# Row sums and row arithmetic in the norms of a transformer kernel, with filler products behind them

## The chip, the cores and the metric

The kernel runs on one core of one Trainium2 chip. The metric is the time of one execution on the device in microseconds (us). It is compared with the time of the changed kernel on the same chip. The engines are named as the profile names them: PE is the matrix engine (PEld its weight loads), DVE the vector engine, ACT the scalar engine, POOL the general engine, and SP issues most DMAs. PSUM is the memory into which PE adds its products, SBUF the memory of everything else.

## The reference

Three transformer blocks in a row, for one sequence of 256 tokens with 1024 features:

```python
def layer_norm(x, g, b):
    mu = jnp.mean(xf, axis=-1, keepdims=True)
    var = jnp.mean(jnp.square(xf - mu), axis=-1, keepdims=True)
    y = (xf - mu) * lax.rsqrt(var + LN_EPS) * g.astype(jnp.float32) + b.astype(jnp.float32)
...
def rms_norm(x, g):
    y = xf * lax.rsqrt(jnp.mean(xf * xf, axis=-1, keepdims=True) + NORM_EPS)
...
# block 1
h = layer_norm(alpha * x + m @ w_out[i], ln1_g[i], ln1_b[i])
f = peer_ffn(h, peer_w_q[i], peer_sub_keys[i], peer_u[i], peer_v[i])
x = layer_norm(alpha * h + f + e, ln2_g[i], ln2_b[i])
# block 2, twice (NSA attention, then forgetting attention)
h = rms_norm(x, norm_g[i, 0])
x = x + rms_norm(m, norm_g[i, 1])
h = rms_norm(x, norm_g[i, 2])
x = x + rms_norm(squared_relu_mlp(h, mlp_w_up[i], mlp_w_down[i]), norm_g[i, 3])
# block 3, twice (mlstm with a gated MLP, then hgrn with a mixture of experts)
hn = rmsnorm(x, norm1_w[layer]) * (1 + scale1) + shift1
x = x + gate1 * y
hn = rmsnorm(x, norm2_w[layer]) * (1 + scale2) + shift2
x = x + gate2 * y
# end
return rmsnorm(x, final_norm_w)
```

Every norm needs, for each of the 256 tokens, the mean of 1024 squares and then one over its square root.

## The kernel before

Features lie on the partitions: an activation is eight tiles of 128 features x 256 tokens, so that a sum over features is a sum over partitions and tiles. A float32 weight is split into two parts (hi on ACT at L316, lo on DVE at L317, 128x1024 at a time), and a product with it is three products on PE (L327 to L329, in `mm3`): hi with hi, hi with the rest of the activation, and lo with hi. Weights come in through SP's queue. A scheduler places all instructions on their engines beforehand, and each engine then takes its own list in order. What follows a norm is therefore late when the norm is late.

A norm goes like this. `Squares.add` squares pairs of tiles on ACT and adds them up on DVE or POOL until two tiles of 128x512 are left. `fold` sums these over the partitions with eight products of one column each (L368): the squares of 128 tokens are the weights, and the result is one number for each token, 128 tokens down the partitions in two columns. `rstd` makes one over the root from these 128x2 numbers: ACT the square root (L376), DVE the variance times -0.5 (L377), the reciprocal (L378), and three more operations (L379 to L381), which are one step of Newton. `spread` (L391) turns the two columns into a row that stands in all partitions, 128x256 in PSUM, by two products. Then the eight tiles of the activation are multiplied with that row: at L453 in `layer_norm`, at L415 in `rms`, at L480 in `add_normed`, where ACT first copies the row to SBUF (L475).

Ten norms have this chain on the way to the next product: two of `layer_norm`, four of `add_normed`, three of `rms` (before mlstm, before its gated MLP, before hgrn), and the last of all. Four more norms are applied late (`inverse`): their products go on with the activation as it is, and the result is multiplied with the row behind. The router (`Router.finish`) uses the two columns as they are. The first layer norm stands at 270 us of the span, the second at 1200, the four of `add_normed` between 1389 and 1943 in attention and MLP in turn, mlstm's at 1942 and hgrn's at 2285, the router at 2473 and the last norm at 2907.

Of the kernel before, what the change touches and what calls it, by code (L numbers as in the profile page):

```python
# [22 lines left out]
T = 256  # L23
# [8 lines left out]
ADDS = 4  # L32
LNV = 8
EPS = (1e-6, 1e-5)
BASE = ("warm", "rs_v", "rs_r", "rs_t", "sqk", "yk", "sq2", "icol")

INV_FREQ = np.float32(10000.0) ** (-np.arange(0, 64, 2, dtype=np.float32) / np.float32(64))

# [178 lines left out]
class Core:  # L217
# [107 lines left out]
    def mm3(self, ps, w, x, start, stop, **k):  # L325
        mm = self.nc.tensor.matmul
        mm(ps, w[0], x[0], start=start, stop=False, **k)  # L327
        mm(ps, w[0], x[1], start=False, stop=False, **k)  # L328
        mm(ps, w[1], x[0], start=False, stop=stop, **k)  # L329

    def lin_chunk(self, src, x, kts=KT, apart=False):

# [61 lines left out]

    def rows_add(self, ps, x, first, last):

        self.nc.tensor.matmul(ps, self.C("onesD"), x, start=first, stop=last)

    def rstd_rows(self, sums, eps):
        return self.spread(self.ms_ps()[:, :T], self.rstd(sums[:, :2], eps))  # L400

    def squares(self, x):
        s = Squares(self)
# [1 line left out]
            s.add(x[:, 2 * j:2 * j + 2])  # L405
        return s

    def rms(self, x, sums, g, b=None, eps=1e-6):

        nc = self.nc  # L410
        r = self.rstd_rows(self.fold(sums), eps)
        hi, lo = self.big([KT, T], F32R, nm="nhi"), self.big([KT, T], F32R, nm="nlo")
        for k in range(KT):
            y = self.small([T], tag="yk", bufs=3)
            nc.vector.scalar_tensor_tensor(y, x[:, k], g[:, k:k + 1], r, op0=OP.mult, op1=OP.mult)  # L415
            if b is None:
                self.split(y, hi[:, k], lo[:, k])
            else:
                nc.scalar.activation(hi[:, k], y, AF.Identity, bias=b[:, k:k + 1])
                nc.vector.scalar_tensor_tensor(lo[:, k], y, b[:, k:k + 1], hi[:, k], op0=OP.add, op1=OP.subtract)  # L420
        return hi, lo
# [11 lines left out]
    def layer_norm(self, r, mean, g, b, g_next=None):  # L433


        nc = self.nc
        sq = Squares(self, nc.vector)
        for k in range(KT):
            nc.vector.tensor_tensor(r[:, k], r[:, k], mean, op=OP.subtract)
            if k % 2:  # L440
                sq.add(r[:, k - 1:k + 1])
        gh, bh = g, b
        if g_next is not None:
            gh, bh = (self.small([KT], tag=t, bufs=1) for t in ("gh", "bh"))
            nc.gpsimd.tensor_tensor(gh, g, g_next, op=OP.mult)
            nc.gpsimd.tensor_tensor(bh, b, g_next, op=OP.mult)
        rs = self.rstd_rows(self.fold(sq), 1e-5)
        hi, lo = (self.big([KT, T], F32R, nm="lhi"), self.big([KT, T], F32R, nm="llo"))
        sq = Squares(self)
        for k in range(KT):  # L450
            y = self.small([T], tag="yk", bufs=3)
            c = slice(k, k + 1)
            nc.vector.tensor_tensor(y, r[:, k], rs, op=OP.mult)  # L453
            nc.scalar.activation(hi[:, k], y, AF.Identity, scale=gh[:, c], bias=bh[:, c])
            eng = nc.vector if k < LNV else nc.gpsimd
            eng.tensor_scalar(r[:, k], y, g[:, c], b[:, c], op0=OP.mult, op1=OP.add)
# [11 lines left out]
    def add_normed(self, x, src, gm, sq, g=None):  # L468

        nc = self.nc
        r = self.rstd_rows(self.fold(sq), 1e-6)
        rs = self.small([T], tag="rsb", bufs=1)
        nc.scalar.activation(rs, r, AF.Copy)  # L475
        nxt = Squares(self, None if g is not None else nc.vector)
        parts = (self.big([KT, T], F32R, nm="nhi"), self.big([KT, T], F32R, nm="nlo")) if g is not None else None
        for k in range(KT):
            m = self.small([T], tag="yk", bufs=3)
            nc.vector.scalar_tensor_tensor(m, src(k), gm[:, k:k + 1], rs, op0=OP.mult, op1=OP.mult)  # L480
            eng = nc.vector if k < ADDS else nc.gpsimd
# [9 lines left out]
        self.nc.scalar.activation(hi, x[:, k], AF.Copy, scale=g[:, k:k + 1])  # L491
        self.nc.vector.scalar_tensor_tensor(lo, x[:, k], g[:, k:k + 1], hi, op0=OP.mult, op1=OP.subtract)  # L492

    def fold(self, sq):

        ps = self.sums()
        n = len(sq.tiles)
        for i, t in enumerate(sq.tiles):
            for f in range(2):
                self.add_sum(ps, 0, t[:, f], i + f == 0, i == n - 1 and f == 1, square=False)  # L500
        return ps

    def inverse(self, sums, eps=1e-6):

        r = self.rstd(sums[:, :2], eps)
        col, row = self.small([2], tag="icol", bufs=1), self.small([T], tag="irow", bufs=1)
        self.nc.vector.tensor_copy(col, r)
        self.nc.scalar.activation(row, self.spread(self.ms_ps()[:, :T], r), AF.Copy)
        return col, row

    def accumulate(self, w, hid, ys, first, last, dts=range(8)):

# [519 lines left out]
def squared_relu(c, x, sq, hs, l, g=None):  # L1032
# [2 lines left out]

    def evac(ps):
        r = c.small([2, T], tag="hr")
        row = inv[0][1][:, None, :].to_broadcast([128, 2, T])
# [53 lines left out]
def nsa(c, x, sq, hs):  # L1092
# [8 lines left out]
    kc, vc = kc[:, 0], kc[:, 1]  # L1101
    K2 = c.big([4, 2, T], nm="K2")
    ps = c.lin_chunk(d["nsa_in"][4], hs)
    col, row = c.inverse(c.fold(sq))
# [193 lines left out]
def fox(c, x, sq, hs):  # L1298
# [4 lines left out]
    pad_heads(c, q)  # L1303
    bf = bcast_row(c, d["rows16"], 0, 16, "bf")
    ps0 = c.lin_chunk(d["fox_in"][0], hs)
    col, row = c.inverse(c.fold(sq))
    row = row[:, None, :].to_broadcast([128, 2, T])
    z, lf = c.small([2, 16], tag="fz", bufs=1), c.small([2, 16], tag="flf", bufs=1)
    ps = small_tok(c, d["fox_f"], 16, hs)
# [115 lines left out]
            nc.vector.tensor_tensor(self.mod[:, l], self.mod[:, l], c.V(f"ada_b{l}"), op=OP.add)  # L1425


def modulated(c, x, sums, w, scale, shift, out=None):
    nc = c.nc
    g = c.small([KT], tag="mg")  # L1430
    nc.vector.scalar_tensor_tensor(g, scale, 1.0, w, op0=OP.add, op1=OP.mult)
    if out is None:
        return c.rms(x, sums, g, shift)
    return c.rms_whole(x, sums, g, shift, out=out)


# [207 lines left out]
def hgrn(c, x, sums, mod):  # L1644
# [120 lines left out]
class Router:  # L1765
# [34 lines left out]

    def finish(self, sq):
        c, nc = self.c, self.c.nc
        r = c.rstd(c.fold(sq)[:, :2], 1e-6)
        lt = c.small([T], tag="lt", bufs=1)
        nc.scalar.activation(lt[:8], self.lg, AF.Copy)
        pt = c.ac_ps()[:, :16].rearrange("p (a e) -> p a e", a=2)
        lg = c.small([2, 8], tag="lg", bufs=1)
        for tt in range(2):
            nc.tensor.transpose(pt[:, tt], lt[:8, tt * 128:tt * 128 + 128], c.C("ident")[:8, :8])
# [13 lines left out]
def places(c, lg):  # L1823
# [27 lines left out]
    nc.vector.tensor_tensor(gt, oh[:, :, 0], oh[:, :, 1], op=OP.add)  # L1851
    ps = c.ms_ps()[:, :8]
    for tt in range(2):
        nc.tensor.matmul(ps, c.C("one"), mk[:, tt], start=tt == 0, stop=tt == 1)
# [182 lines left out]
```

## Time and profile before

| | |
|---|---|
| times of three runs, us | 2934.7, 2927.17, 2935.34 |
| their median, us | 2934.7 |
| the profiled execution, us | 2925.78 |
| its span from the first to the last instruction, us | 2924.1 |
| mean granted clock of PE in it | 0.975 |

The profile shows one execution. Its span is the time between its first and its last instruction, and 1.7 us lie around it. The granted clock is told for any stretch as a share of the full 2.4 GHz; 0.50 is the half level of 1.2 GHz. A product in the trace is two records where its operands are full float32, and a record's duration is longer than its distance to the next one, as they are pipelined.

### The profile page before, as it was taken

Reading aid. Unit: us, or ns where it says so; the run is one execution under the profiler, and the core shown is the slowest. Engines: PE = TensorE matmul, PEld = TensorE weight load, DVE = VectorE, ACT = ScalarE, POOL = GpSimd, SP = SyncE. Lnnn points to the kernel's source line nnn. Section 1 sums busy time; section 2 is a strip of 40 time slices with the busy share of each in tenths; the row PEclk is TensorE's granted clock in tenths of the full one; section 3 lists DMA queues with packets and bytes.
Section 4 is the critical chain, followed back from the end, with each engine's and each line's share of the span. In section 5 each row is a group of like instructions: output and inputs, shape, how many; then the busy total and the mean of one; then the engine's idle time right before and its main releaser. Section 6 shows DMA issues by size and latency. Waiting matters only on the chain. (4 is left out here: it accounts for less than half of the span.)

```text
span 2924.1 us, 51291 instructions
## 1 busy us (share of the span) xinstructions
PE 2818.6 (96%) x20880; PEld 2666.6 (91%) x20880; DVE 2063.4 (71%) x3757; ACT 1543.8 (53%) x2196; POOL 156.8 (5%) x137
## 2 busy tenths in 40 slices
PE   8999999899999999999999999989999998999998
PEld 8998989899999999887999989989899997888886
DVE  6655979777777785667655565565655696899997
ACT  5454317544444444457444464445544645777775
POOL 0000000000000000210001000001000170000000
PEclk9999999999999999899999999989999999999998
DMA  7543346888888786341454415534255432789885
GB/s 277 209 155 136 134 144 231 288 302 297 299 302 298 283 300 230 123 176 47 145 185 146 173 59 188 182 108 159 102 188 188 141 129 87 295 331 336 324 331 211
DMA packets 118901, 602.23 MB, mean 206 GB/s; under 512 B 10752, under 2 KB 46080, under 8 KB 49664
## 3 DMA queue, kind: packets, MB, share of 16 engines
q1 hardware_dynamic: 78480, 557.96, 53.1%
q10 hardware_dynamic: 40176, 40.91, 4.4%
q8 instruction: 166, 2.72, 0.4%
q14 instruction: 79, 0.65, 0.1%
HBM read 579.43 MB, written 19.39 MB: 205 GB/s over the span
## 5 line engine op out<-in xcount | busy, mean ns | idle before, releaser
L317 DVE TENSOR_TENSOR lo<-raw,hi 128x1024 fp32r<-128x1024 f32 x915 | 1126.2, 1244 | 590.4 <-ACT hi L316 586.9
L316 ACT ACTIVATE hi<-raw 128x1024 fp32r<-128x1024 f32 x915 | 960.9, 1057 | 926.5 <-PE mm L328 507.5
L327 PE MATMUL mm<-nhi,hi 128*128 128x256 f32 x1312 | 378.6, 290 | 10.2 <-ACT nhi L491 6.8
L328 PE MATMUL mm<-nlo,hi 128*128 128x256 f32 x1312 | 378.9, 289 | 0.5 <-DVE nlo L492 0.5
L329 PE MATMUL mm<-nhi,lo 128*128 128x256 f32 x1312 | 376.7, 287 | 0.0
L329 PE MATMUL mm<-lhi,lo 128*128 128x256 f32 x1024 | 295.1, 288 | 7.7 <-DVE lo L317 7.7
L327 PE MATMUL mm<-lhi,hi 128*128 128x256 f32 x1024 | 294.9, 289 | 5.1 <-ACT r L933 2.8
L328 PE MATMUL mm<-llo,hi 128*128 128x256 f32 x1024 | 295.6, 289 | 0.0
L328 PE MATMUL ac<-r,hi 128*128 128x256 f32 x1024 | 288.2, 282 | 0.0
L329 PE MATMUL ac<-r,lo 128*128 128x256 f32 x1024 | 288.0, 281 | 0.0
L327 PE MATMUL ac<-r,hi 128*128 128x256 f32 x1024 | 287.7, 281 | 0.0
L327 PEld LDWEIGHTS mm<-nhi,hi 128*128 128x128 f32 x1312 | 257.5, 197 | 12.2 <-ACT nhi L491 7.5
L328 PEld LDWEIGHTS mm<-nlo,hi 128*128 128x128 f32 x1312 | 257.7, 197 | 2.5 <-DVE nlo L492 1.7
L329 PEld LDWEIGHTS mm<-nhi,lo 128*128 128x128 f32 x1312 | 257.7, 197 | 0.1
L329 PEld LDWEIGHTS mm<-lhi,lo 128*128 128x128 f32 x1024 | 201.0, 196 | 9.0 <-DVE lo L317 8.1
L327 PEld LDWEIGHTS mm<-lhi,hi 128*128 128x128 f32 x1024 | 201.2, 197 | 6.9 <-ACT r L933 3.0
L328 PEld LDWEIGHTS mm<-llo,hi 128*128 128x128 f32 x1024 | 200.9, 196 | 1.1 <-issue 0.7
L328 PE MATMUL ac<-hlo,hi 128*128 128x256 f32 x688 | 193.0, 281 | 0.0
L328 PEld LDWEIGHTS ac<-r,hi 128*128 128x128 f32 x1024 | 192.9, 188 | 0.0
L327 PE MATMUL ac<-hhi,hi 128*128 128x256 f32 x688 | 192.8, 280 | 0.0
L329 PEld LDWEIGHTS ac<-r,lo 128*128 128x128 f32 x1024 | 192.7, 188 | 0.0
L327 PEld LDWEIGHTS ac<-r,hi 128*128 128x128 f32 x1024 | 192.7, 188 | 0.0
(590 smaller groups left out, 6288.9 us busy)
## 6 DMA issues: line engine op xcount, KB each, us to landing
raw<-in_moe_gu SPq DMA_DIRECT2D x88, 1024.0 KB, 5.1
raw<-in_peer_u SPq DMA_DIRECT2D x64, 1024.0 KB, 5.0
raw<-in_peer_v SPq DMA_DIRECT2D x64, 1024.0 KB, 5.5
raw<-in_ada SPq DMA_DIRECT2D x48, 1024.0 KB, 7.2
raw<-in_moe_d SPq DMA_DIRECT2D x40, 1024.0 KB, 5.5
raw<-in_up SPq DMA_DIRECT2D x32, 1024.0 KB, 4.9
raw<-in_down SPq DMA_DIRECT2D x32, 1024.0 KB, 4.9
raw<-in_ffn_gu SPq DMA_DIRECT2D x22, 1024.0 KB, 4.9
```

Source lines behind the costliest of these rows:

```text
L316: nc.scalar.activation(hi, raw[:, a:a + m], AF.Copy)
L317: nc.vector.tensor_tensor(lo, raw[:, a:a + m], hi, op=OP.subtract)
L327: mm(ps, w[0], x[0], start=start, stop=False, **k)
L328: mm(ps, w[0], x[1], start=False, stop=False, **k)
L329: mm(ps, w[1], x[0], start=False, stop=stop, **k)
```

## The change

The sums of `fold` are made with a full matrix of ones (over the number of features) as weights and the squares as the moving side, as L397 did for the means of the layer norm: four products of 128x256, and the result is the row, already in all partitions. The arithmetic behind it (`rstd_rows`, L413 to L419 of the changed file) runs on that row, 128x256 in place of 128x2. `spread` is gone there, and so is the copy at L475. `inverse` gives only the row; where a column is wanted as well (two of its four calls), `column` makes it with two products of one column. The router keeps the old way (`fold_cols`, `rstd`).

`busy` is new: it puts a number of products behind the product recorded last (`issue_after` fixes that order), with constants on both sides, into the unused half of a PSUM bank, and nobody reads them. In `layer_norm` there are 9 ahead of the sums and 7 behind them, in `add_normed` 8 behind them, or 20 where the next norm follows with no product between (the last MLP), in `rms` 7 behind them and before hgrn 7 ahead of them too, in the router 9 behind the transposes and 5 in the part that counts the tokens of each expert. `inverse` and the last norm have none.

```diff
     def rows_add(self, ps, x, first, last):
-        self.nc.tensor.matmul(ps, self.C("onesD"), x, start=first, stop=last)
-
-    def rstd_rows(self, sums, eps):
-        return self.spread(self.ms_ps()[:, :T], self.rstd(sums[:, :2], eps))
+        self.pe = self.nc.tensor.matmul(ps, self.C("onesD"), x, start=first, stop=last)
+
+    def busy(self, ps, n):
...
+        with self.tc.issue_after(self.pe.ins):
+            for _ in range(n):
+                self.nc.tensor.matmul(ps[:, 256:512], self.C("ident"), self.cst[:, 0:256], start=True, stop=True)
+
+    def rstd_rows(self, sums, eps, more=0, out=None):
...
+        v, r, t = (self.small([T], tag=g, bufs=1) for g in ("rr_v", "rr_r", "rr_t"))
+        m = sums[:, :T]
+        nc.scalar.activation(t, m, AF.Sqrt, bias=self.C(eps))
+        nc.vector.tensor_scalar(v, m, eps, -0.5, op0=OP.add, op1=OP.mult)
+        nc.vector.reciprocal(r, t)
+        nc.vector.tensor_tensor(t, r, r, op=OP.mult)
+        nc.vector.tensor_tensor(t, t, v, op=OP.mult)
+        out = r if out is None else out
+        nc.vector.scalar_tensor_tensor(out, t, 1.5, r, op0=OP.add, op1=OP.mult)
+        if more:
+            self.busy(self.ms_ps(), more)
+        return out
...
-        r = self.rstd_rows(self.fold(sums), eps)
+        r = self.rstd_rows(self.fold(sums, wait), eps, 7)
...
-        rs = self.rstd_rows(self.fold(sq), 1e-5)
+        rs = self.rstd_rows(self.fold(sq, 9), 1e-5, 7)
...
-        r = self.rstd_rows(self.fold(sq), 1e-6)
-        rs = self.small([T], tag="rsb", bufs=1)
-        nc.scalar.activation(rs, r, AF.Copy)
+        rs = self.rstd_rows(self.fold(sq), 1e-6, 20 if g is None else 8)
...
-    def fold(self, sq):
+    def fold(self, sq, wait=0):
+
+        ps = self.ms_ps()
+        self.busy(ps, wait)
+        n = len(sq.tiles)
+        for i, t in enumerate(sq.tiles):
+            for f in range(2):
+                self.rows_add(ps[:, :T], t[:, f], i + f == 0, i == n - 1 and f == 1)
+        return ps
...
-        r = self.rstd(sums[:, :2], eps)
-        col, row = self.small([2], tag="icol", bufs=1), self.small([T], tag="irow", bufs=1)
-        self.nc.vector.tensor_copy(col, r)
-        self.nc.scalar.activation(row, self.spread(self.ms_ps()[:, :T], r), AF.Copy)
-        return col, row
+        return self.rstd_rows(sums, eps, out=self.small([T], tag="irow", bufs=1))
+
+    def column(self, row):
+
+        ps = self.ms_ps()[:, :2]
+        for i in range(2):
+            self.nc.tensor.matmul(ps[:, i:i + 1], row[:, i * 128:i * 128 + 128], self.C("ident")[:, :1], start=True, stop=True)
+        col = self.small([2], tag="icol", bufs=1)
+        self.nc.vector.tensor_copy(col, ps)
+        return col
...
-    hs = modulated(c, x, sums, c.V("n1w1"), mod[:, 1, 8:16], mod[:, 1, 0:8])
+    hs = modulated(c, x, sums, c.V("n1w1"), mod[:, 1, 8:16], mod[:, 1, 0:8], wait=7)
...
-        r = c.rstd(c.fold(sq)[:, :2], 1e-6)
+        r = c.rstd(c.fold_cols(sq)[:, :2], 1e-6)
...
+            c.pe = nc.tensor.transpose(pt[:, tt], lt[:8, tt * 128:tt * 128 + 128], c.C("ident")[:8, :8])
+        c.busy(c.ac_ps(), 9)
...
-    nc = bacc.Bacc("TRN2", target_bir_lowering=False, num_devices=1, dynamic_dma_scratch_size=8192)
+    nc = bacc.Bacc("TRN2", target_bir_lowering=False, num_devices=1, dynamic_dma_scratch_size=4096)
```

PE, the first layer norm, before: the means (L397), the sums of squares (L368), the spreading (L391) and the first products behind the norm (L327).

```order
L397 MATMUL ms_2637<-x,cst 128x256 x4
L368 MATMUL ms_2908<-cst,sq_342_2889 128x1 x4
L368 MATMUL ms_2908<-cst,sq_346_2905 128x1 x4
L391 MATMUL ms_2917<-cst,rs_r_2919 128x128 x2
L327 MATMUL mm_3000<-lhi_2929,hi_2992 128x256
```

PE, the same place in the changed kernel; L406 are the fillers, L397 now also the sums.

```order
L397 MATMUL ms_2637<-x,cst 128x256 x4
L406 MATMUL ms_2908<-cst 128x256 x9
L397 MATMUL ms_2908<-sq_342_2889,cst 128x256 x2
L397 MATMUL ms_2908<-sq_346_2905,cst 128x256 x2
L406 MATMUL ms_2931<-cst 128x256 x7
L327 MATMUL mm_3010<-lhi_2939,hi_3002 128x256
```

Eight sums of one column have become four of 256, the two products of the spreading have gone, and sixteen fillers stand around the sums; the first product behind the norm follows the last filler.

PE, from the last MLP of block 2 into mlstm, before: the sums of the MLP's norm, its spreading, and the same for mlstm's norm.

```order
L368 MATMUL ms_20569<-cst,sq_2946_20556 128x1 x4
L368 MATMUL ms_20569<-cst,sq_2950_20566 128x1 x4
L391 MATMUL ms_20578<-cst,rs_r_20580 128x128 x2
L368 MATMUL ms_20635<-cst,sq_2959_20598 128x1 x4
L368 MATMUL ms_20635<-cst,sq_2969_20626 128x1 x4
L391 MATMUL ms_20644<-cst,rs_r_20646 128x128 x2
L327 MATMUL mm_20706<-nhi_20656,hi_20698 128x256
```

The same place in the changed kernel.

```order
L397 MATMUL ms_20559<-sq_2939_20546,cst 128x256 x2
L397 MATMUL ms_20559<-sq_2943_20556,cst 128x256 x2
L406 MATMUL ms_20573<-cst 128x256 x20
L397 MATMUL ms_20637<-sq_2951_20600,cst 128x256 x2
L397 MATMUL ms_20637<-sq_2961_20628,cst 128x256 x2
L406 MATMUL ms_20651<-cst 128x256 x7
L327 MATMUL mm_20709<-nhi_20659,hi_20701 128x256
```

Twenty fillers stand between the two norms, and mlstm's sums can't start before the last of them.

DVE, hgrn's norm, before: L1773 is arithmetic of hgrn's modulation, L377 to L381 are `rstd`, L317 is the low part of a weight chunk, L415 the first use of the norm.

```order
L1773 SCALAR_TENSOR_TENSOR mg_25789<-mod,vecs 128x8
L377 TENSOR_SCALAR rs_v_24364<-ms_24354 128x2
L378 RECIPROCAL rs_r_24365<-rs_t_24366 128x2
L379 TENSOR_TENSOR rs_t_24366<-rs_r_24365 128x2
L380 TENSOR_TENSOR rs_t_24366<-rs_t_24366,rs_v_24364 128x2
L381 SCALAR_TENSOR_TENSOR rs_r_24365<-rs_t_24366,rs_r_24365 128x2
L317 TENSOR_TENSOR lo_24478<-raw_24471,hi_24477 128x1024
L415 SCALAR_TENSOR_TENSOR yk_24377<-x,mg_24352,ms_24363 128x256
```

The same place in the changed kernel (L414 to L419 are the arithmetic on rows, L437 the first use).

```order
L1810 SCALAR_TENSOR_TENSOR mg_25801<-mod,vecs 128x8
L414 TENSOR_SCALAR rr_v_24370<-ms_24358 128x256
L415 RECIPROCAL rr_r_24371<-rr_t_24372 128x256
L317 TENSOR_TENSOR lo_24490<-raw_24483,hi_24489 128x1024
L416 TENSOR_TENSOR rr_t_24372<-rr_r_24371 128x256
L417 TENSOR_TENSOR rr_t_24372<-rr_t_24372,rr_v_24370 128x256
L419 SCALAR_TENSOR_TENSOR rr_r_24371<-rr_t_24372,rr_r_24371 128x256
L437 SCALAR_TENSOR_TENSOR yk_24389<-x,mg_24356,rr_r_24371 128x256
```

The split of the weight chunk has moved from behind the norm's arithmetic to behind the reciprocal, ahead of the three operations that finish the norm. It waits for ACT's half of the same chunk (L316). The order of SP is the same in both kernels.

## Rows read from the trace of the kernel before

**Rows 1.** Page: busy time of the matrix engine, its share of the span, instructions.

```profile
PE 2818.6 (96%) x20880; PEld 2666.6 (91%) x20880; DVE 2063.4 (71%) x3757; ACT 1543.8 (53%) x2196; POOL 156.8 (5%) x137
```

**Rows 2.** Timelines, both layer norms: start us, duration us, engine, line, operation, count, [idle before].

```profile
273.36 3.17 PE L368 MATMUL ms<-cst,sq 128*128 128x1 f32 x16 [3.98 <-DVE sq L565]
276.56 0.26 ACT L376 ACTIVATE rs_t<-ms,cst 128x2 f32<-128x2 f32 x1 [2.13 <-PE ms L368]
278.99 0.75 DVE L453 TENSOR_TENSOR yk<-x,ms 128x256 f32<-128x256 f32 x2 [1.32 <-PE ms L391]
...
1203.26 3.57 PE L368 MATMUL ms<-cst,sq 128*128 128x1 f32 x16 [3.83 <-DVE sq L565]
```

**Rows 3.** Windows: length, busy (instructions) of PE, PEld, DVE, ACT, POOL; clock; DMA.

```profile
1450.00:1500.00 50.00, 50.00 (x422) 50.00 (x421) 27.44 (x26) 22.71 (x26) 0.00 (x0) 1.00 0.54 188
280.10:284.07 3.97, 3.97 (x17) 3.79 (x18) 3.97 (x13) 2.19 (x5) 0.00 (x0) 0.50 0.00 0
1210.41:1215.91 5.50, 5.50 (x24) 5.26 (x25) 5.50 (x15) 3.72 (x7) 1.28 (x1) 0.50 0.00 0
1949.62:1953.19 3.57, 3.57 (x15) 3.43 (x16) 3.57 (x10) 2.05 (x5) 0.00 (x0) 0.50 0.00 0
...
2291.94:2297.94 6.00, 6.00 (x27) 5.86 (x28) 4.52 (x12) 2.05 (x5) 0.00 (x0) 0.50 0.43 164
```

**Rows 4.** Timeline of the matrix engine in the MLP after the first attention.

```profile
1399.80 1.05 PE L368 MATMUL ms<-cst,sq 128*128 128x1 f32 x8 [0.84 <-POOL sq L565]
```

**Rows 5.** Timeline of the matrix engine: means before the second layer norm.

```profile
1195.82 3.62 PE L397 MATMUL ms<-x,cst 128*128 128x256 f32 x16
```

**Rows 6.** Timeline of the hgrn norm, all engines.

```profile
2284.79 3.54 PE L368 MATMUL ms<-cst,sq 128*128 128x1 f32 x16 [3.03 <-DVE sq L565]
...
2289.61 1.23 DVE L317 TENSOR_TENSOR lo<-raw,hi 128x1024 fp32r<-128x1024 f32 x1
...
2290.86 1.26 DVE L415 SCALAR_TENSOR_TENSOR yk<-x,mg,ms 128x256 f32<-128x256 f32 x3
```

**Rows 7.** Groups of 128x256: operation, count | busy us, mean ns | idle before.

```profile
L741 ACT ACTIVATE sgm<-mm,vecs 128x256 f32<-128x256 f32 x16 | 6.7, 463 | 0.0
...
L453 DVE TENSOR_TENSOR yk<-x,ms 128x256 f32<-128x256 f32 x16 | 6.0, 414 | 2.6 <-PE ms L391 2.6
```

**Rows 8.** Groups of the reciprocals on the vector engine, same columns.

```profile
L378 DVE RECIPROCAL rs_r<-rs_t 128x2 f32<-128x2 f32 x15 | 2.3, 155 | 0.0
...
L378 DVE RECIPROCAL rs_r<-rs_t 128x8 f32<-128x8 f32 x4 | 0.8, 194 | 0.0
...
L1193 DVE RECIPROCAL cst<-cst 128x16 f32<-128x16 f32 x2 | 0.5, 253 | 0.1
```

**Rows 9.** Timelines and windows of two bare waits, in the experts and in hgrn.

```profile
550.28 0.58 PE L327 MATMUL mm<-lhi,hi 128*128 128x256 f32 x1 [2.76 <-ACT r L933]
...
2402.08 2.02 PE L1729 MATMUL ac<-X 128*128 128x128 f32 x16 [1.74 <-DVE A L1730]
...
550.32:553.73 3.41, 3.41 (x16) 3.41 (x17) 0.00 (x0) 1.34 (x2) 0.00 (x0) 0.50 1.16 293
2400.33:2410.00 9.67, 7.46 (x63) 7.30 (x63) 9.67 (x11) 1.69 (x2) 6.21 (x3) 1.00 0.31 109
```

**Rows 10.** Windows behind the chunk products of two of three inverses.

```profile
1222.74:1226.15 3.41, 3.41 (x18) 3.41 (x18) 2.36 (x7) 1.34 (x3) 3.41 (x3) 0.50 0.02 6
...
1601.62:1608.45 6.83, 6.83 (x34) 6.06 (x34) 2.75 (x9) 1.70 (x3) 2.46 (x3) 0.50 0.30 121
```

**Rows 11.** Timeline of the matrix engine, last MLP to mlstm.

```profile
1929.70 2.00 PE L368 MATMUL ms<-cst,sq 128*128 128x1 f32 x16
...
1942.40 3.55 PE L368 MATMUL ms<-cst,sq 128*128 128x1 f32 x16 [7.32 <-DVE sq L565]
```

**Rows 12.** Timeline of the matrix engine in the router.

```profile
2473.02 0.38 PE L1809 MATMUL ac<-cst,lt 8*128 8x8 f32 x2
2477.78 0.61 PE L1838 MATMUL ms<-mk,cst 128*128 128x16 f32 x2 [4.38 <-DVE mk L1835]
```

More of the change, by code (lines that the diff above doesn't have):

```diff
@@ L34 @@
 EPS = (1e-6, 1e-5)
-BASE = ("warm", "rs_v", "rs_r", "rs_t", "sqk", "yk", "sq2", "icol")
+BASE = ("warm", "rs_v", "rs_r", "rs_t", "rr_v", "rr_r", "rr_t", "sqk", "yk", "sq2", "icol")
 INV_FREQ = np.float32(10000.0) ** (-np.arange(0, 64, 2, dtype=np.float32) / np.float32(64))
@@ L328, in mm3 @@
         mm(ps, w[0], x[1], start=False, stop=False, **k)
-        mm(ps, w[1], x[0], start=False, stop=stop, **k)
+        self.pe = mm(ps, w[1], x[0], start=False, stop=stop, **k)
     def lin_chunk(self, src, x, kts=KT, apart=False):
@@ L395, in rows_add @@
     def rows_add(self, ps, x, first, last):
-        self.nc.tensor.matmul(ps, self.C("onesD"), x, start=first, stop=last)
-    def rstd_rows(self, sums, eps):
-        return self.spread(self.ms_ps()[:, :T], self.rstd(sums[:, :2], eps))
+        self.pe = self.nc.tensor.matmul(ps, self.C("onesD"), x, start=first, stop=last)
+    def busy(self, ps, n):
+        if not n:
+            return
+        with self.tc.issue_after(self.pe.ins):
+            for _ in range(n):
+                self.nc.tensor.matmul(ps[:, 256:512], self.C("ident"), self.cst[:, 0:256], start=True, stop=True)
+    def rstd_rows(self, sums, eps, more=0, out=None):
+        nc = self.nc
+        v, r, t = (self.small([T], tag=g, bufs=1) for g in ("rr_v", "rr_r", "rr_t"))
[10 more added lines that the diff above has]
+        return out
     def squares(self, x):
@@ L406, in squares, with rms @@
         return s
-    def rms(self, x, sums, g, b=None, eps=1e-6):
+    def rms(self, x, sums, g, b=None, eps=1e-6, wait=0):
         nc = self.nc
-        r = self.rstd_rows(self.fold(sums), eps)
+        r = self.rstd_rows(self.fold(sums, wait), eps, 7)
         hi, lo = self.big([KT, T], F32R, nm="nhi"), self.big([KT, T], F32R, nm="nlo")
@@ L492, in scaled, with fold_cols @@
         self.nc.vector.scalar_tensor_tensor(lo, x[:, k], g[:, k:k + 1], hi, op0=OP.mult, op1=OP.subtract)
-    def fold(self, sq):
+    def fold(self, sq, wait=0):
[6 more added lines that the diff above has]
+        return ps
+    def fold_cols(self, sq):
         ps = self.sums()
@@ L1037, in evac @@
         r = c.small([2, T], tag="hr")
-        row = inv[0][1][:, None, :].to_broadcast([128, 2, T])
+        row = inv[0][:, None, :].to_broadcast([128, 2, T])
         nc.vector.scalar_tensor_tensor(r, ps, 0.0, row, op0=OP.max, op1=OP.mult)
@@ L1103, in nsa @@
     ps = c.lin_chunk(d["nsa_in"][4], hs)
-    col, row = c.inverse(c.fold(sq))
+    row = c.inverse(c.fold(sq))
+    col = c.column(row)
     rv = rp.rearrange("p (a t) -> p a t", a=4)
@@ L1305, in fox @@
     ps0 = c.lin_chunk(d["fox_in"][0], hs)
-    col, row = c.inverse(c.fold(sq))
+    row = c.inverse(c.fold(sq))
+    col = c.column(row)
     row = row[:, None, :].to_broadcast([128, 2, T])
@@ L1425, in step, with modulated @@
             nc.vector.tensor_tensor(self.mod[:, l], self.mod[:, l], c.V(f"ada_b{l}"), op=OP.add)
-def modulated(c, x, sums, w, scale, shift, out=None):
+def modulated(c, x, sums, w, scale, shift, out=None, wait=0):
     nc = c.nc
@@ L1432, in modulated @@
     if out is None:
-        return c.rms(x, sums, g, shift)
+        return c.rms(x, sums, g, shift, wait=wait)
     return c.rms_whole(x, sums, g, shift, out=out)
@@ L1808, in finish @@
         for tt in range(2):
-            nc.tensor.transpose(pt[:, tt], lt[:8, tt * 128:tt * 128 + 128], c.C("ident")[:8, :8])
+            c.pe = nc.tensor.transpose(pt[:, tt], lt[:8, tt * 128:tt * 128 + 128], c.C("ident")[:8, :8])
+        c.busy(c.ac_ps(), 9)
         for tt in range(2):
@@ L1853, in places @@
     for tt in range(2):
-        nc.tensor.matmul(ps, c.C("one"), mk[:, tt], start=tt == 0, stop=tt == 1)
+        c.pe = nc.tensor.matmul(ps, c.C("one"), mk[:, tt], start=tt == 0, stop=tt == 1)
+    c.busy(c.ac_ps(), 5)
     most = c.hold([1], "most")
```

## The prediction

> **What bounds the kernel now.** I read the page first, then the windows and timelines at the norms. PE is busy for 2818.6 us of a span of 2924.1 [rows 1], so only two things about PE can be worth time: where it stands still, and where its records are slow. Both happen at the norms. In an undisturbed stretch 422 products take 50 us, 0.1185 each, at granted clock 1.00; behind hgrn's norm 27 take 6.00 at clock 0.50, 0.222 each [rows 3], and later 34 take 6.83, 0.201 each [rows 10]. I take 0.213 between these: a product at the half level of 1.2 GHz in place of the full 2.4 costs 0.095 us more. The reader is to see in the timelines that ahead of the first norm PE waits 3.98 us for the last squares, that its sums then take 3.17 us, and that the first use of the norm comes 2.46 us after their end at 276.53 [rows 2]. In this stretch nothing else stands in PE's list. The norm's arithmetic is a chain in which each engine waits for the last.
>
> **A. The chain behind the sums.** Before: 2.46 us from the end of the sums to the first use in the first layer norm [rows 2], with two products of spreading in it. After: square root, variance, reciprocal and three more operations, all on 128x256, on the result of the sums, with no spreading. The root takes 0.46 by a 128x256 ACT row, the multiplications and the variance 0.41 to 0.42 by a 128x256 DVE row [rows 7] and by the three of 1.26 us in hgrn [rows 6]. The reciprocal has no row of this shape. Its three shapes take 155 ns for 2 columns, 194 for 8 and 253 for 16 [rows 8]: 6.5 ns a column over the first step, 7.4 over the second. Bounds from rows: 0.41 (it streams like a multiplication) and 0.155 + 254 x 7.4 ns = 2.03. I take 6.7 ns, low in the second group of rows since the first step rests on 19 instructions and the last on two: 1.86 us. Five hops between operations at about 0.04 (the root starts 0.03 after the sums end [rows 2]), less 0.08 of overlap between variance and reciprocal (an estimate), give 0.46 + 0.41 + 1.86 + 3 x 0.42 + 0.20 - 0.08 = 4.11, so +1.65 per norm. In hgrn the order puts a weight split of 1.23 [rows 6] into the chain ahead of the last three operations; that split stood ahead of the first use before as well, but under the spreading's products. There the chain was 2288.33 to 2290.86, 2.53, and becomes 4.11 + 1.23 + 0.04 = 5.38: +2.85. Nine norms at 1.65 and this one: **+17.7**.
>
> By the Trainium skill, "VectorE: DVE Perf Modes", section "First, the fixed hardware budget", the reciprocal is an iterative divide with a repeat count of 8; with the 0.96 GHz of its section "Specifications" that is 8.3 ns a column, as an estimate from that page 2.27 us, and by it the sum would be 4.1 higher. The rows above, at 6.5 to 7.4 ns, say the same kind of thing with a smaller size, and the sum goes by them.
>
> **B. The sums.** A full float32 product 128x256 is two records; the 16 records of the means take 3.62 us at the full clock [rows 5], (3.62 - 0.38) / 15 = 0.216 apart, taking 0.38 for the last one, so 0.43 a product, and four take 1.73 + 0.16. Where fillers run ahead of the sums (9 x 0.43 = 3.9 in a wait of 3.98 in the first layer norm, 3.83 in the second, 7 x 0.43 = 3.0 in 3.03 before hgrn) the sums should run at full clock: 1.89 against 3.17, 3.57 and 3.54 [rows 2, 6], that is 1.3 + 1.7 + 1.65 = **-4.65**. Ahead of mlstm's norm 20 fillers start when the MLP's sums end, 1929.70 + 1.89 = 1931.6, and take 20 x 0.43, to 1940.3; mlstm's sums came at 1942.40 [rows 11] and will come 1.65 later, so PE stands bare for 3.7 us and I count nothing (at full clock it would be 3.55 - 1.89 = 1.65).
>
> **C. The products behind the norm.** In five norms PE is full behind the first product, at clock 0.50: 17, 24, 15, 15 (one of two such windows is shown) and 27 products [rows 3], 98 x 0.095 = 9.3 us to be had if the clock stays up. Seven fillers last 3.0 us from the end of the sums; the first real product comes 4.11 + 1.1 (from first use to first product, 278.99 to 280.10 [rows 2, 3]) = 5.2 later, so PE still stands bare for 2.2, and in hgrn for 3.4. What is bare time worth? After 2.76 us of it the clock stood at 0.50 for the next 3.4 us; after 1.74 us it stayed at 1.00 [rows 9]. Ours lie between, or next to the worse one. I count half: **-4.65**. In the four norms of `add_normed` PE waits for the adders behind the norm (one such wait is 0.84 for POOL [rows 4]), so that a fast PE waits longer there: nothing.
>
> **D. Second falls.** Behind three inverses, some 12 to 14 us after the norm, the clock fell once more for 3.41, 3.41 and 6.83 us [rows 10] (the one of 3.41 not shown is like the first), 13.65 us in all, of which 1 - 0.1185 / 0.213 = 0.44, 6.1 us, is to be had. With less waiting ahead of them some of these should not come; no row shows why they come so late, so I count two thirds by choice: **-4.1**.
>
> **E. The router.** PE waits 4.38 us there [rows 12]. Nine fillers take 3.9 at full clock and 7.8 at half: from 2473.40 to 2481.2, past 2477.78, which would cost 3.4. If the clock comes up, the router's own small products, 0.61 for two, gain about 1 between them by estimate. I take **+1**, nearer to the fillers that fit.
>
> **Counted at nothing.** The inverses' longer arithmetic (2.9 us more on DVE each, four times) lies beside chunk products that run meanwhile: DVE is busy for 2.75 of 6.83 us there [rows 10]; if that cover is gone it is up to 1.6 each, since PE has that much less work ahead. `column` is two products of some 0.3 us under the same cover. The smaller scratch for DMA descriptors and the unchanged SP order move no weight transfer that I can see; PE idles next to nothing on weights.
>
> **Sum.** 17.7 - 4.65 - 4.65 - 4.1 + 1 = +5.3. On the profiled execution's 2925.78 (2924.1 of span and 1.7 around it) that is 2931.1. That execution is faster than all three timed runs: 8.9 below their median of 2934.7. The mean of all four is 2930.7, and with +5.3 on it I forecast **2936**. 0.3% is 8.8 us; that is about what a measurement can tell from no change here.
>
> **The rivals.**
> - *The clock holds everywhere.* Then C gives all 9.3, D all 6.1, mlstm's sums 1.65 more and the router -1: 17.7 - 6.3 - 9.3 - 6.1 - 1 = -5.0, so 2925.7. For it: fillers make the bare stretches shorter than the ones before. Against it: 2.2 to 3.7 us stay bare in the norms, with the fall after 2.76 as the nearest row [rows 9]. Chance 0.17.
> - *The reciprocal does not grow with the row.* At 0.41 it saves 1.45 in ten norms: -14.5, so 2921.5, and with the first rival together about 2911. For it: a multiplication does 256 columns in 0.41 [rows 7]. Against it: three shapes that lie on one line [rows 8]. Chance 0.13.
> - *The fillers run out and the clock falls as before* (the other side). C and D give nothing, the router's fillers run at half and cost 3.4: 17.7 - 4.65 + 3.4 = +16.5, so 2947. If the 20 fillers ran at half too, they would last 17.2 us to 1948.8, against the arrival at 1944.05, +4.7 more: 2952. It decides when less than about 1.2 of C's and D's 8.75 comes back: the sum passes +12.8 then, 0.3% over the median. For it: fillers are placed right behind the sums, when the clock is already up, and end ahead of the wait's end. Against it: they halve the wait. Chance 0.25.
>
> The forecast itself has 0.45. Faster by over 0.3% is the second rival and half of the first, 0.20; slower is the third, 0.25; no change to tell is 0.55. The range is 2920 to 2950: below it lie the first two rivals together, above it the slow twenty fillers; it takes in the reciprocal's upper bound (0.17 x 10 = +1.7) and the bare inverses (up to 6.4).
>
> **What would show it.** The reciprocal on 128x256 at 1.8 to 1.9 us, the chain from the sums to first use at 4.1 (hgrn 5.4); the sums of the layer norms at 1.9; the clock of the stretches behind the five norms, 0.50 in some and 1.00 in others; the falls behind the inverses in one place of three; the router's fillers ending at 2477 or 2481. The prediction is wrong if the reciprocal lasts 0.4, if the clock stays up through bare waits of 2 to 4 us, or if the time is lost at a place that I don't name, such as DVE's weight splits behind the longer chains in the inverses.

## The result: slower by 0.57%

| | before | changed |
|---|---|---|
| median of 4 runs, us | 2933.66 | 2947.73 |
| lowest and highest, us | 2927.17, 2935.34 | 2945.34, 2951.21 |
| ratio, 95% interval | | 1.0057 (1.0039 to 1.0074) |
| span of the profiled execution, us | 2924.1 | 2947.5 |
| mean granted clock | 0.975 | 0.984 |

By medians the change costs 14.1 us (the ratio, which is not that of the medians, would make it 17), 2.7 times the forecast's 5.3 and just under the third rival's 16.5, at a higher mean clock. First the page of the changed kernel, the row that answers to [rows 1]:

```profile
PE 2856.1 (97%) x20956; PEld 2689.2 (91%) x20956; DVE 2096.3 (71%) x3755; ACT 1544.1 (52%) x2188; POOL 157.7 (5%) x137
```

PE is busy for 37.5 us more. The groups by line and shape say with what: 236 records of fillers (L406), 55.0 us. All other products together take 17.5 us less.

```profile
L406 PE MATMUL ms<-cst 128*128 128x256 f32 x208 | 47.1, 380 | 0.0
...
L406 PE MATMUL ac<-cst 128*128 128x256 f32 x28 | 7.9, 444 | 0.0
...
L415 DVE RECIPROCAL rr_r<-rr_t 128x256 f32<-128x256 f32 x14 | 24.4, 1743 | 0.0
```

The reciprocal takes 1.74 us, against 0.155 for two columns [rows 8]. The timeline of the first layer norm, which answers to [rows 2]:

```profile
269.24 4.05 PE L406 MATMUL ms<-cst 128*128 128x256 f32 x18
273.38 1.99 PE L397 MATMUL ms<-sq,cst 128*128 128x256 f32 x8
275.21 3.19 PE L406 MATMUL ms<-cst 128*128 128x256 f32 x14
275.41 0.47 ACT L413 ACTIVATE rr_t<-ms,cst 128x256 f32<-128x256 f32 x1 [0.95 <-PE ms L397]
275.91 0.42 DVE L414 TENSOR_SCALAR rr_v<-ms 128x256 f32<-128x256 f32 x1 [2.26 <-ACT rr_t L413]
276.26 1.74 DVE L415 RECIPROCAL rr_r<-rr_t 128x256 f32<-128x256 f32 x1
...
279.41 0.76 DVE L475 TENSOR_TENSOR yk<-x,rr_r 128x256 f32<-128x256 f32 x2
...
280.52 0.67 PE L327 MATMUL mm<-lhi,hi 128*128 128x256 f32 x2 [2.13 <-ACT lhi L476]
```

It goes as forecast: the sums take 1.99 at the full clock, the chain from their end (275.37) to the first use 4.04, and PE is bare for 2.13 behind the last filler. Before, the same first product stood at 280.10: shorter sums and the longer chain nearly cancel out, 0.42 us remain. Now the windows at the half level behind the five norms of term C, which answer to [rows 3] (columns as there):

```profile
280.70:284.11 3.41, 3.39 (x15) 3.10 (x16) 3.41 (x12) 1.62 (x4) 0.00 (x0) 0.50 0.02 5
1212.54:1215.95 3.41, 3.41 (x18) 3.41 (x18) 3.41 (x8) 2.54 (x5) 1.86 (x1) 0.50 0.00 0
1966.88:1970.29 3.41, 3.41 (x19) 3.41 (x18) 2.71 (x7) 1.30 (x4) 0.00 (x0) 0.50 0.02 5
2117.07:2120.48 3.41, 3.41 (x19) 3.41 (x18) 2.70 (x7) 1.30 (x4) 0.00 (x0) 0.50 0.00 0
2315.05:2318.46 3.41, 3.39 (x15) 3.24 (x16) 3.41 (x10) 2.08 (x5) 0.00 (x0) 0.50 0.52 219
```

The clock still falls behind every one of these norms, with 15 + 18 + 19 + 19 + 15 = 86 products at half in place of 98. C gave 12 x 0.095 = 1.1 us of its 9.3 (by the length of the windows, 17.0 us in place of 22.4, about 2.4). The larger loss is at a place that the sum has at nothing, the four inverses. The vector engine and PE in the inverse of the first attention (1229.40 to 1242.87), then the vector engine in that of the first MLP, then PE there (1415.47), in the forgetting attention (1617.48) and in the second MLP (1770.82):

```profile
1229.40 1.22 DVE L1142 TENSOR_TENSOR rope<-rope,irow 128x1024 f32<-128x1024 f32 x1
...
1235.31 7.45 DVE L1162 TENSOR_TENSOR win<-kvc,vecs 64x240 f32<-64x240 f32 x8
...
1242.87 1.57 PE L1172 MATMUL ac<-raw,win 128*64 128x256 f32 x6 [1.95 <-POOL rraw L1039]
...
1408.99 1.23 DVE L317 TENSOR_TENSOR lo<-raw,hi 128x1024 fp32r<-128x1024 f32 x1 [2.85 <-ACT hi L316]
1410.14 0.42 DVE L414 TENSOR_SCALAR rr_v<-ms 128x256 f32<-128x256 f32 x1
1410.47 1.75 DVE L415 RECIPROCAL rr_r<-rr_t 128x256 f32<-128x256 f32 x1
1412.25 0.43 DVE L416 TENSOR_TENSOR rr_t<-rr_r 128x256 f32<-128x256 f32 x1
1412.59 1.22 DVE L317 TENSOR_TENSOR lo<-raw,hi 128x1024 fp32r<-128x1024 f32 x1
1413.73 0.41 DVE L417 TENSOR_TENSOR rr_t<-rr_t,rr_v 128x256 f32<-128x256 f32 x1
1414.18 0.42 DVE L419 SCALAR_TENSOR_TENSOR irow<-rr_t,rr_r 128x256 f32<-128x256 f32 x1
1414.64 1.29 DVE L1074 SCALAR_TENSOR_TENSOR hr<-mm,irow 128x512 f32<-128x512 f32 x2
...
1415.47 0.36 PE L327 MATMUL mm<-nhi,hi 128*128 128x256 f32 x1 [1.31 <-DVE hr L1074]
...
1617.48 0.58 PE L541 MATMUL ms<-cst,irow 128*128 128x1 f32 x4 [3.18 <-DVE irow L419]
...
1770.82 0.35 PE L327 MATMUL mm<-nhi,hi 128*128 128x256 f32 x1 [1.32 <-DVE hr L1074]
```

In the first attention the rotation tables (`rope`, L1142) are multiplied with the row, the keys need the tables, and eight additions (L1162) need the keys. PE waits 1.95 us at the product that reads their result. The view names POOL as the releaser, but that instruction had ended at 1241.86; the last of the additions ended at 1242.76, 0.11 ahead of PE's start, and fits. In the MLP one weight split stands ahead of the arithmetic on DVE and one between its parts, the row is ready 5.6 us after the first of them begins, and PE waits 1.31 us for the first chunk to leave PSUM. In the forgetting attention the column's two products (L541) stand in PE's own list ahead of chunk products, and PE waits 3.18 us for the row. None of these waits is in either profile of the kernel before or in that of run 4, which has the old inverses. The four make 7.8 us.

### The profile page after: what moved, and what is told of

Same layout as the page of the kernel before. It is cut to its first block, busy times and chain, and to the rows that moved or that the text cites. A ratio compares the mean times of both kernels' runs of the same rounds, so it can differ in the third digit from the quotient of the medians.

```text
span 2947.5 us, 51423 instructions
## 1 busy us (share of the span) xinstructions
PE 2856.1 (97%) x20956; PEld 2689.2 (91%) x20956; DVE 2096.3 (71%) x3755; ACT 1544.1 (52%) x2188; POOL 157.7 (5%) x137
## 5 line engine op out<-in xcount | busy, mean ns | idle before, releaser
L317 DVE TENSOR_TENSOR lo<-raw,hi 128x1024 fp32r<-128x1024 f32 x915 | 1123.9, 1242 | 603.2 <-ACT hi L316 599.4
L316 ACT ACTIVATE hi<-raw 128x1024 fp32r<-128x1024 f32 x915 | 960.5, 1057 | 943.1 <-PE mm L328 508.3
L327 PE MATMUL mm<-nhi,hi 128*128 128x256 f32 x1312 | 376.5, 288 | 19.1 <-ACT nhi L511 9.3
L327 PE MATMUL mm<-lhi,hi 128*128 128x256 f32 x1024 | 293.5, 287 | 5.6 <-ACT lhi L476 4.3
L327 PE MATMUL ac<-r,hi 128*128 128x256 f32 x1024 | 287.7, 281 | 0.0
L327 PEld LDWEIGHTS mm<-nhi,hi 128*128 128x128 f32 x1312 | 255.2, 195 | 22.9 <-ACT nhi L511 11.2
L329 PEld LDWEIGHTS mm<-lhi,lo 128*128 128x128 f32 x1024 | 199.8, 195 | 11.1 <-DVE lo L317 10.2
L327 PEld LDWEIGHTS mm<-lhi,hi 128*128 128x128 f32 x1024 | 199.5, 195 | 7.6 <-ACT lhi L476 5.1
L327 PEld LDWEIGHTS ac<-r,hi 128*128 128x128 f32 x1024 | 192.7, 188 | 0.0
L329 PE MATMUL ac<-hhi,lo 128*128 128x256 f32 x688 | 192.4, 280 | 0.0
```

Of the source, the lines that this page charges most:

```text
L316: nc.scalar.activation(hi, raw[:, a:a + m], AF.Copy)
L317: nc.vector.tensor_tensor(lo, raw[:, a:a + m], hi, op=OP.subtract)
L329: self.pe = mm(ps, w[1], x[0], start=False, stop=stop, **k)
```

## The experiments

Ratios are to the kernel before on the same chip, whose median was 2932.14 us in the first group of runs (1, 3, 4, 7), 2933.23 in the second (2, 5, 6, 12) and 2929.82 in the third (8 to 11, on another chip than the first two). All runs made from the change, and run 6, also have its smaller scratch for DMA descriptors (4096 in place of 8192), the others have not; no run tests that by itself.

**1. Fillers alone, in the banks of the norm.** The kernel before, with (the helper `busy` and the numbers at the calls are left out)

```diff
...
+    def rstd_rows(self, sums, eps, mid=0, more=0):
+        self.busy(sums, mid)
+        r = self.rstd(sums[:, :2], eps)
+        ps = self.ms_ps()
+        row = self.spread(ps[:, :T], r)
+        self.busy(ps, more)
+        return row
...
```

> The kernel before with fillers alone: the arithmetic stays on 128x2 and in every norm fillers are put around it in numbers that fit its shorter waits (9 or 7 ahead of the sums as in the change, 2 between the sums and the spreading, 2 to 5 behind it, 4 and 16 between the last MLP and mlstm; none in the router and the inverses). Theory (the row arithmetic costs, the fillers give back): faster than before by what the sums, the products behind the norms and the second falls give back, 8 to 15 us, so 2919 to 2926. Rival (the fillers themselves cost, by standing ahead of work in the matrix engine's list): not faster than before, 2932 to 2942.

Measured: 2962.63 us, 1.0110 (1.0087 to 1.0133). It is the slowest but one, and neither the theory nor the rival had it. The timeline of its first layer norm:

```profile
275.17 1.95 PE L368 MATMUL ms<-cst,sq 128*128 128x1 f32 x16
276.97 1.11 PE L405 MATMUL ms<-cst 128*128 128x256 f32 x4
278.12 0.26 ACT L376 ACTIVATE rs_t<-ms,cst 128x2 f32<-128x2 f32 x1 [1.88 <-PE ms L405]
279.29 0.76 PE L391 MATMUL ms<-cst,rs_r 128*128 128x128 f32 x4 [1.21 <-DVE rs_r L381]
279.84 1.92 PE L405 MATMUL ms<-cst 128*128 128x256 f32 x4
281.79 0.75 DVE L466 TENSOR_TENSOR yk<-x,ms 128x256 f32<-128x256 f32 x2 [2.56 <-PE ms L405]
```

The square root and the first use wait for the last filler (L405) in the bank that they read, though it writes the other half. The fillers lie inside the chain instead of beside it. The changed kernel has none there: its fillers behind the sums take a bank of their own.

**2. Fillers alone, in banks that nobody is about to read.** As 1, with the bank of the spreading for the fillers ahead of it, and that of the sums behind it:

```diff
-        self.busy(sums, mid)
-        r = self.rstd(sums[:, :2], eps)
         ps = self.ms_ps()
+        self.busy(ps, mid)
+        r = self.rstd(sums[:, :2], eps)
         row = self.spread(ps[:, :T], r)
-        self.busy(ps, more)
+        self.busy(sums, more)
```

> Fillers alone again, in the same places and numbers, but never in a bank that somebody is about to read: those ahead of the spreading go into the bank of the spreading, those behind it into the bank of the sums, which has been read by then. Theory: in the run before, the root and the first use waited for the last filler in their bank; with that gone the fillers give back about what they gave the change (4 us between the change with and without them), so 2926 to 2930. Rival: 9 to 13 as the forecast had it, 2919 to 2923. Other rival: fillers cost in any bank, 2935 and more.

Measured: 2922.13 us, 0.9967 (0.9954 to 0.9980): 11 us faster than before, inside the rival's 9 to 13. In its first layer norm the square root starts 0.03 us behind the sums (274.21 + 1.95), and PE is bare for 0.28 ahead of the first product:

```profile
276.19 0.26 ACT L376 ACTIVATE rs_t<-ms,cst 128x2 f32<-128x2 f32 x1 [0.90 <-PE ms L368]
...
279.22 0.51 PE L327 MATMUL mm<-lhi,hi 128*128 128x256 f32 x2 [0.28 <-ACT lhi L467]
```

With the arithmetic on columns, fillers give back nearly what the forecast's B, C and D held (13.4). Its windows behind the first two norms, mlstm's and hgrn's stand at the full clock:

```profile
278.00:283.00 5.00, 4.54 (x33) 3.88 (x32) 4.89 (x15) 2.66 (x5) 0.00 (x0) 1.00 0.01 3
1207.00:1213.00 6.00, 5.69 (x43) 5.31 (x44) 6.00 (x17) 5.09 (x10) 1.29 (x1) 1.00 0.01 3
1948.00:1953.00 5.00, 4.86 (x40) 4.60 (x39) 4.59 (x12) 3.02 (x7) 0.00 (x0) 1.00 0.02 5
...
2290.00:2295.00 5.00, 4.86 (x39) 4.66 (x40) 4.41 (x12) 3.00 (x7) 0.00 (x0) 1.00 0.54 200
```

**3. The change without fillers.**

```diff
     def busy(self, ps, n):
+        return
```

> The change without any filler: the row sums and the arithmetic on 128x256 alone. Theory: slower than the change by what the fillers gave back, 9 to 15 us, so 2956 to 2963. Rival (the fillers cost): as fast as the change or faster, 2938 to 2948.

Measured: 2951.68 us, 1.0061 (1.0040 to 1.0082). By medians the fillers of the change give back 4 us, not the 9 to 15 expected. The intervals of this run and of the change overlap, so that even the 4 are not shown.

**4. The change with the old inverses.**

```diff
     def inverse(self, sums, eps=1e-6):
-        return self.rstd_rows(sums, eps, out=self.small([T], tag="irow", bufs=1))
+        r = self.rstd(sums[:, :2], eps)
...
+        self.nc.scalar.activation(row, self.spread(self.ms_ps()[:, :T], r), AF.Copy)
+        return col, row
```

> The change, but the four inverses as before (columns, arithmetic on 128x2, spreading, copy). Theory (the inverses that the forecast counted at nothing cost some 11 us in the profile): 2934 to 2939. Rival (they are covered, and the loss of the profile there is a clock that happened to fall elsewhere): 2945 to 2950.

Measured: 2941.52 us, 1.0033 (1.0019 to 1.0046). The inverses cost 6.2 us in the change. That lies between the two expectations, about half of the 11 that the change's profile had shown against the first profile of before.

**5. The old inverses and no fillers.** The diffs of 3 and 4 together: only the ten norms are on rows.

> The change without fillers and with the old inverses: only the ten norms are on rows. By the sum of the forecast 17.7 over the kernel before, 2950; by adding up the runs so far (the change less 6 for the inverses, plus 4 for the fillers) 2945. If the norms' chain is partly hidden: under 2942.

Measured: 2949.43 us, 1.0065 (1.0043 to 1.0087). The ten norms cost 16.2 us by medians (13 to 26 by the interval), against 17.7 in the forecast's A. The fillers give back 7.9 of it when the inverses are the old ones (2949.43 to 2941.52).

**6. Only the inverses on rows.** The kernel before, with the row arithmetic in `inverse` alone and `column` behind it, and no fillers:

```diff
-    col, row = c.inverse(c.fold(sq))
+    row = c.inverse(c.fold_rows(sq))
+    col = c.column(row)
```

> The kernel before with only the four inverses on rows (row sums, arithmetic on 128x256, column made from the row); no norm is touched and there are no fillers. Theory (the inverses are on the path): 6 to 11 us over the kernel before, 2938 to 2943. Rival (their cost came with the fillers or with the later norms): 2932 to 2935.

Measured: 2941.93 us, 1.0036 (1.0023 to 1.0049), 8.7 us over the kernel before. They are on the path without any filler too. Its profile has PE's waits at the same four places: 2.65 us in the first attention, 1.02, 3.18 and 1.31. The smaller scratch is in this run as well, but it loses nothing by itself ahead of the inverses: ACT's last weight split ahead of the second layer norm, at 1197 us, ends 0.1 us later than before, and those behind the wait in the first attention, from 1255 us, end 4.2 later.

**7. The reciprocal twice.**

```diff
         nc.vector.reciprocal(r, t)
+        nc.vector.reciprocal(r, t)
```

> The change with the reciprocal on 128x256 made twice in a row. If each of them is on the path that sets the end, a second one costs 1.75 us in ten norms and in three or four inverses: 2947.7 + 17 to 25, so 2965 to 2973. If the inverses are covered: +17, 2965. If the reciprocal is hidden by other waits: under 2953.

Measured: 2982.39 us, 1.0173 (1.0153 to 1.0192): 35 us over the change, where 14 more reciprocals of 1.74 are 24.4. That is more than any of the three expectations: they cost more than their own time, so nothing hides them on the whole. In the first MLP PE's wait for the same instruction grows from 1.31 to

```profile
1424.97 0.55 PE L327 MATMUL mm<-nhi,hi 128*128 128x256 f32 x1 [4.04 <-DVE hr L1075]
```

That is 2.73 us more, and not 1.74 alone: in this kernel's list two weight splits stand between the reciprocals and the last two steps, where there was one. The products behind the wait run at half (0.41 us a record in place of 0.28).

**8. The column later.** The change, with `column` in the forgetting attention behind the small product whose result it scales:

```diff
-    col = c.column(row)
...
     ps = small_tok(c, d["fox_f"], 16, hs)
+    col = c.column(irow)
```

> The change with the column of the forgetting attention made from the row later, behind the small product that it is needed for, so that the matrix engine no longer waits 3.15 us for the inverse there. If this wait is what that inverse costs: 2 to 3.5 us under the change, 2944 to 2946. If the wait moves to the next product, which needs a bank that the inverse's row must free: under 1 us, 2947 to 2949.

Measured: 2940.41 us, 1.0031 (1.0019 to 1.0042), 7 us under the change where 2 to 3.5 were expected. In its profile PE's wait there is 1.07 in place of 3.18:

```profile
1620.30 0.36 PE L327 MATMUL mm<-nhi,hi 128*128 128x256 f32 x1 [1.07 <-DVE fq L1360]
```

That is the part expected. The rest can't be put on this edit: the clock inside mlstm (run 12) stayed up in its profile, and the medians of the kernel before that go with the two lie 3.8 us apart. Each against its own, this run costs 10.6 us and the change 14.1, which leaves 3.5.

**9. The change without the 8 fillers of `add_normed`.**

```diff
-        rs = self.rstd_rows(self.fold(sq), 1e-6, 20 if g is None else 8)
+        rs = self.rstd_rows(self.fold(sq), 1e-6, 20 if g is None else 0)
```

> The change without the 8 fillers behind the norms of add_normed. If they cost there with the row arithmetic as well: 3 to 8 us under the change, 2940 to 2945. If they gain, or the longer chain leaves nothing to lose: 2947 to 2951.

Measured: 2941.70 us, 1.0037 (1.0026 to 1.0049). 6 us under the change by medians, 0.2 points by ratio, with intervals that overlap. Each against its own kernel before, it is 11.9 us and 14.1. No gain of these fillers shows; that they cost is not shown either.

**10 and 11. Fillers alone, less those of `add_normed`; then with the router's.** As 2, with none in the three norms of `add_normed` that a weight product follows; and that with 9 and 5 fillers in the router as in the change:

```diff
-        r = self.rstd_rows(self.fold(sq), 1e-6, 2 if g is not None else 4, 16 if g is None else 5)
+        r = self.rstd_rows(self.fold(sq), 1e-6, 0 if g is not None else 4, 16 if g is None else 0)
...
+        c.busy(c.ac_ps(), 9)
...
+    c.busy(c.ac_ps(), 5)
```

> The run with fillers in banks of their own, less the fillers of the three norms of add_normed that a weight product follows (they stay between the last MLP and mlstm). Theory: in those stretches the adders on POOL set the end, a fast matrix engine only waits longer for them and bare, and falls later in the stretch that it fills itself; its profile loses some 9 us between the second layer norm and the last MLP. Without them 2914 to 2918. Rival (they gain as everywhere else): 2924 to 2928.

> The same with the router's fillers of the change (9 behind the transposes and 5 behind the counts, in a bank that nobody reads). The change's profile gained 2.1 us behind the router against the kernel before: so 2 under the run without them, 2912 to 2916. Rival (the forecast's +1 to +3.4: the fillers outlast the wait): 2916 to 2920.

Measured: 2922.44 us, 0.9971 (0.9958 to 0.9984), and 2919.88 us, 0.9964 (0.9950 to 0.9978). The first of these lies between its two expectations. By ratio, dropping those fillers changes next to nothing with columns (0.9967 and 0.9971); by medians, each against its own kernel before, 11.1 us of gain become 7.4, so that a small loss isn't excluded. The last one is the fastest of all, 10 us under the kernel before. It is 2.6 us under the one without the router's fillers, as its theory has it, but that lies within the intervals.

**12. The kernel before once more.** No edit.

> The kernel before once more, for a second profile of it: whether the clock falls at the same places (16 stretches, 147 us in the first profile), and in particular whether the stretch inside mlstm at about 2054 to 2075, which ran at the full clock before and at half in the change with the same instructions, can fall in the kernel before too. If the places move from run to run, the 23 us between the two profiles hold several us of this; if they are fixed, all of it is the change's.

Measured: 2933.48 us, one run. The window in which the clock fell inside mlstm, in this second profile, and the same stretch of instructions (with a margin) in the first one of before:

```profile
2053.57:2070.64 17.07, 15.96 (x67) 14.79 (x68) 6.73 (x26) 6.56 (x14) 0.00 (x0) 0.50 0.01 2
```

```profile
2050.00:2067.00 17.00, 13.54 (x100) 12.08 (x99) 8.66 (x37) 10.56 (x20) 0.00 (x0) 1.00 0.01 2
```

The same kernel ran this stretch at half in one execution and at full in the other. Between the two profiles 7.7 us lie (spans of 2931.8 and 2924.1), so 23 us between the first profile of before and that of the change overstate the change by about that much.

## Why the prediction was wrong

**A, the chain, was right**: 4.04 us against 4.11 in the first layer norm, and 16.2 us for ten norms (run 5) against 17.7. The clock is hardly a part of this: PE stood at half for 162 us in that run's profile, for 147 and 163 in the two of before. The reciprocal was forecast at 1.86 and took 1.74, (1743 - 155) / 254 = 6.25 ns a column, just under the lowest slope of [rows 8]. The estimate from the repeat count of 8 of the Trainium skill, "VectorE: DVE Perf Modes", section "First, the fixed hardware budget", was 2.27; the row decides, and it is smaller. In hgrn the split did move into the chain, which took 5.0 from the sums' end at 2309.00 (2307.01 + 1.99) to first use, 0.4 less than forecast:

```profile
2311.55 1.16 DVE L317 TENSOR_TENSOR lo<-raw,hi 128x1024 fp32r<-128x1024 f32 x1
...
2313.99 1.28 DVE L437 SCALAR_TENSOR_TENSOR yk<-x,mg,rr_r 128x256 f32<-128x256 f32 x3
```

**B was right** (1.99 for the sums in the first layer norm against 1.89). **E had the wrong sign, by the profile**: the router's fillers last 5.53 us and end about a microsecond after the wait that they fill, but that microsecond is lost to nobody: the first products of the gathering for the experts (L1936) come 8.8 us behind the transposes (L1846), as in the kernel before, and the clock is up from there. Between the products ahead of the router and those behind it the change gains 2 us on the profile before. PE there:

```profile
2496.23 0.38 PE L1846 MATMUL ac<-cst,lt 8*128 8x8 f32 x2
2496.54 5.53 PE L406 MATMUL ac<-cst 128*128 128x256 f32 x18
2501.91 0.29 PE L1876 MATMUL ms<-mk,cst 128*128 128x16 f32 x2
...
2505.03 0.60 PE L1936 MATMUL ac<-pm,xhi 128*128 128x256 f32 x3
```

**"Counted at nothing" is the step that failed.** It held that the inverses' longer arithmetic lies beside chunk products and that DVE has room. Room was the wrong measure. The arithmetic is a chain of steps in a list that is fixed beforehand; the splits between its steps make it longer than its own durations, and PE's next chunk needs a PSUM buffer that only the inverse's row can empty. In the first MLP the row was ready 3.9 us behind the sums before (1403.62 to 1407.53) and is 6.2 behind them now (1408.41 to 1414.60). The products cover a part of the 2.3 more, and 1.31 is left as PE's wait. That is the sign of being wrong that the prediction itself names last. Its price for bare inverses, 1.6 each or 6.4 in all, is close to the 6.2 us of run 4 and the 8.7 of run 6, but partly by luck: the four waits differ (1.95, 1.31, 3.18 and 1.32), and they come from the chain and the order of the lists, where the price was taken from PE's shorter sums. What the forecast also did not follow is the column: `column` was called two products under the same cover, but PE takes its list in order and waited 3.18 us at them (rows above). With them later in the list (run 8) 1.07 was left.

**C and D came in part.** In the change C's places gave 1.1 to 2.4 us. D's falls last 10.24 us (three of 3.41, at 1243.26, 1605.07 and 1618.73) where they lasted 13.65 [rows 10], and two of the three begin behind a wait for an inverse (1242.87 and 1617.48). With the old inverses (run 4's profile) there are 13.6 us at half in C's places and 3.41 in D's: by the prediction's share of 0.44 that is 3.9 and 4.5 us, near its 4.65 and 4.1. So half and two thirds were not far off where no inverse stood in the way, though they were choices. The runs show 7.9 us for all fillers there, with some 5 us of uncertainty, against 12.4 in the sum (B, C and D less E). If it is less, a part is lost again at other waits; where is not shown. In the change only 4 are left, and the profiles show a reason, a PE that comes earlier and waits longer for the row: without fillers (run 3) the four waits are 0, 1.31, 1.00 and 1.31, 3.6 us in all, and with them 7.8.

With columns the fillers give 11 (run 2), at four of the same five places at the full clock; there PE was bare for 0.2 to 0.3 us ahead of the first product in the first layer norm, and in the change for 2.1. In the change and in run 4 the five places are bare for 2.0 to 3.1 us, and nine of these ten waits have the half level behind them. Of the two rows on bare waits, the worse one was the nearer, as the text had said. And a gain in PE is kept only up to the next wait for somebody else. Ahead of the experts' tables the changed kernel's PE was 1.2 us earlier (549.06 against 550.28 in [rows 9]), and then waited 6.33 for a weight split where it had waited 4.16. Of the 1.2 us 0.56 was left:

```profile
558.76 0.58 PE L329 MATMUL mm<-lhi,lo 128*128 128x256 f32 x1 [6.33 <-DVE lo L317]
```

```profile
559.32 0.58 PE L329 MATMUL mm<-lhi,lo 128*128 128x256 f32 x1 [4.16 <-DVE lo L317]
```

(the second is the kernel before).

By medians the account is 16.2 for the norms, 7.9 back for the fillers, 6.2 for the inverses: +14.5, against 14.1 measured. Against the sum, the inverses make 6.2 more than nothing, the fillers give 4.5 less, and the norms cost 1.5 less. The third rival (2947) had the time and half of the cause: C and D gave little in the change, as it said, but its router cost nothing, the twenty fillers ran at the full clock in 8.80 us, and what made up for that were the inverses. Its threshold (less than about 1.2 of C's and D's 8.75) was worked out with the router at +1; with its own +3.4 it is 3.7.

```profile
1944.70 8.80 PE L406 MATMUL ms<-cst 128*128 128x256 f32 x40
```

**What stays open.** The parts don't add up in every order: inverses cost 8.7 alone and 6.2 in the change, but hardly 2 without fillers (runs 3 and 5). PE's waits at the four inverses, 8.2, 7.8 and 3.6 us in the profiles of these kernels, go the same way, but each is one profile, and each difference has about 5 us of uncertainty. What the smaller scratch does by itself was not measured; the 6.2 is between kernels that both have it, the 16.2 and the 8.7 are not. What decides in which executions the clock falls inside mlstm was not tried.

## What to carry to other kernels

Arithmetic on few numbers should stay on few: a reciprocal over 256 columns costs eleven times one over two, and saving the product that spreads the result didn't pay for it here. Whether longer work is hidden is asked at the instruction that waits for its result, with everything that stands between its steps on its engine, and not from that engine's busy share. Fillers that hold the clock up were worth their place beside the chain, in a bank that no step of the chain reads, and cost in one that it reads. That they pay only where the stretch behind them is PE's own is read from the waits; no run separates it.

## What the runs showed of the hardware

- The reciprocal's time grew with the columns by 6.25 ns each from 2 (155 ns) to 256 (1743 ns), when a multiplication of 256 takes 422 ns in the same chain.
- Fillers in the unused half of a PSUM bank held up a reader of the other half to their end: behind 1.11 us of them the root started 1.00 us after the sums' last product (277.12 to 278.12, run 1) instead of 0.03 (run 2). Whether the chip or the program's own semaphores impose that was not separated.
- The granted clock of one and the same stretch differs between executions of one kernel: 0.50 and 1.00 inside mlstm.
